# Early even differences, a third pair in turns, and a plain chunk placed elsewhere in a two-layer trunk's ConvFFN

## The chip, the cores and the metric

One core of one Trainium2 chip. The metric is the device time of one execution in microseconds (us), the median of several runs.

## What is computed

A trunk of two layers on 512 tokens of 1024 features, in float32. Layer 0 is a Mamba-2 mixer, layer 1 a differential attention with shared keys and values; behind each stands a ConvFFN, and the change lies in these two.

```python
def conv_ffn(x, ln_g, up_w, conv_w, conv_b, down_w):
    u = causal_dwconv(rms_norm(x, ln_g) @ up_w, conv_w, conv_b)   # 3 taps along the tokens
    gate, up = u[..., :FFN_DIM], u[..., FFN_DIM:]                 # FFN_DIM = 2816
    return (jax.nn.silu(gate) * up) @ down_w
```

## The kernel before

**Products.** float32 products run on TensorE in three passes: each operand is split into a rounded high part (ScalarE) and the rest, its low part (VectorE), and high times high, high times low and low times high are summed in PSUM. Weights come by chunks of 128 x 1024 numbers (512 KB). `chunk(key)` emits loads and splits up to two chunks ahead of the one in use; the tiles `wr` (raw), `wh` and `wl` (high and low) have three buffers each. `plan` lists the chunks in the order of their use.

**Who sets the order.** TensorE runs its instructions in the order of the program. The order of the other engines and of the DMA queues is laid out when the kernel is built, by a planner that takes the program's order as priority and estimates times; an instruction that is ready early can be placed far ahead of its place in the code. Each engine then runs its list strictly in order.

**The up projection.** The 2816 features of gate and of up form 22 pairs of 128 columns each: pair p is gate block p and up block p. Parts `PARTS_D` hold pairs 0-5, 6-13 and 14-21. Two neighbouring pairs form a double. A plain double ("P" in `KINDS`) takes four chunks, gate and up of each pair, in 24 products of 512 tokens each (three passes over eight blocks of x). A double of kind "S" is multiplied in seven half-size products by a Strassen scheme, "5126734", each with 24 products of 256 columns (12 for each of two column blocks); the sums of weights that it needs are added by DMA into the raw tile (`up_plus`, on GpSimd's queue) after an earlier of the seven has read it. `STEPS[i]` is the order of the steps of part i: P a plain chunk, a digit a step of the Strassen double, D the down projection of the part before. Part 1 has two plain doubles (pairs 6-7, 10-11) and two Strassen ones (8-9, 12-13).

**Start of the ConvFFN.** Pairs 0 and 1 are multiplied by x before its norm is known (the row `nr` is multiplied in at evacuation). For the others x is normalised and split in four quarters, `split_whole`: blocks 0 and 2, 1 and 3, then 4 and 6, 5 and 7 (`xgh`, `xgl`). Pairs below `WHOLE` are multiplied in turns: the first chunk holds blocks 0-3 of x's features for the gate columns and the up columns, the second blocks 4-7 for both, so that two PSUM banks grow together. Pairs from `WHOLE` on take the gate chunk with all eight blocks, then the up chunk. `x_sums` forms the sums of x for the Strassen doubles in `sE` and `sO`.

**After a pair.** `taps` forms the three-tap convolution (one ScalarE pass, two VectorE passes) for gate and up, Silu is taken on ScalarE, `gated` multiplies (line 1160) and calls `operands`. The down projection is a Strassen scheme too: of each double it needs seven sides of 256 tokens, split in high and low (`pieces`): side 0 from the even pair, sides 1 to 6 once the odd pair is gated. In layer 0 these are the even pair's difference and the mixed differences and sums, in the tiles `sh` and `sl`; in parts with eight pairs the last double puts them in the tiles of `sE`, which the trace then names `sEh` and `sEl`. `down_features` (layer 0) takes the steps "5126743" with sides 3, 0, 1, 6, 4, 5, 2: the even pair's difference comes first, with 24 products for each of its two chunks in parts of eight pairs.

**Staging.** In layer 0, `stage()` is called once per step and moves key weights for layer 1: at every second call it either loads a tile (SyncE's queue) or scales it on ScalarE (line 1011) and sends it to DRAM (ScalarE's queue). There are eight such tiles, one buffer.

## Time and profile before

| | us |
|---|---|
| median of 3 runs | 1331.74 (1331.48 to 1332.08) |
| profiled execution | 1334.15 |
| its span, first to last instruction | 1332.5 |
| TensorE busy | 1312.7 (99% of the span), mean granted clock 0.992 |
| VectorE busy | 1072.4 (80%) |
| ScalarE busy | 745.8 (56%) |

Lines with L are lines of the kernel. In a wait "X <- Y", engine and tile X stood idle until Y had ended. In rows in order of time, the bracket at the end gives the idle time before the instruction and what ended it.

### The profile page before, as it was taken

The numbers are of one execution on the slowest core, as the hardware profiler recorded it, in microseconds if no ns is written. First come the engines' busy times: TensorE is split into PE (matmuls) and PEld (weight loads), VectorE is DVE, ScalarE is ACT, GpSimd is POOL, SyncE is SP. The second block draws the span as 40 slices with busy tenths as digits, with TensorE's granted clock in tenths as the row PEclk, the third lists the DMA queues.
The fourth block names the chain that finished last, engine by engine and source line by source line (L and its number), as shares of the span: only waits on it lengthen the run. The fifth ranks groups of instructions, "written<-read, shape, count | busy, mean of one in ns | idle before, by whom it ended". The sixth has DMA issues, their size and how long they took to land.

```text
span 1332.5 us, 18904 instructions
## 1 busy us (share of the span) xinstructions
PE 1312.7 (99%) x7059; PEld 1112.0 (83%) x7059; DVE 1072.4 (80%) x1785; ACT 745.8 (56%) x1223; POOL 185.2 (14%) x212
## 2 busy tenths in 40 slices
PE   9999999999999999999998999999999999999998
PEld 8878888888887899889888988778787889978887
DVE  7989888789878977786766969677779978897777
ACT  6696554742456635553444676777656545553442
POOL 4230300300120421011002310000020031011001
PEclk9999999999998999999998999999999999999999
DMA  7553433432365797468336583222143487456335
GB/s 206 158 156 92 143 106 106 140 95 72 118 192 177 169 230 165 121 127 205 98 92 111 162 165 116 80 64 79 49 119 92 114 209 170 127 112 204 95 64 126
DMA packets 198524, 174.18 MB, mean 131 GB/s; under 512 B 7900, under 2 KB 172128, under 8 KB 198432
## 3 DMA queue, kind: packets, MB, share of 16 engines
q1 hardware_dynamic: 164272, 119.68, 30.2%
q0 software_dynamic: 30704, 47.99, 18.8%
q10 hardware_dynamic: 3456, 5.30, 1.1%
q8 instruction: 55, 0.90, 0.3%
q14 instruction: 37, 0.30, 0.1%
HBM read 166.51 MB, written 6.44 MB: 130 GB/s over the span
## 4 chain that ended last, share of the span: by engine, by line
PE 91%; DVE 5%; ACT 2%; DMA 1%; issue 1%; DVEq 0%; ACTq 0%; SPq 0%
PE ps_in L246 5%; PE ps_in L248 5%; PE ps_in L247 5%; PE ps_g L247 4%; PE ps_g L248 4%; PE ps_g L246 4%; PE ps_u L246 4%; PE ps_u L247 4%; PE ps_u L248 4%; PE ps_s L1434 3%; PE ps_s L1439 3%; PE ps_s L1437 3%; PE ps_s L1333 2%; PE ps_s L1336 2%; PE ps_s L1338 2%; PE ps_o L247 2%
## 5 line engine op out<-in xcount | busy, mean ns | idle before, releaser
L196 DVE TENSOR_TENSOR wl_h<-wr_h,wh_h 128x1024 fp32r<-128x1024 f32 x72 | 88.5, 1231 | 47.8 <-ACT wh_h L185 45.2
L246 PE MATMUL ps_in<-xgh,wh_in 128*128 128x512 f32 x304 | 122.9, 404 | 0.0
L248 PE MATMUL ps_in<-xgh,wl_in 128*128 128x512 f32 x304 | 119.7, 394 | 0.0
L247 PE MATMUL ps_in<-xgl,wh_in 128*128 128x512 f32 x304 | 119.1, 392 | 0.0
L185 ACT ACTIVATE wh_h<-wr_h 128x1024 fp32r<-128x1024 f32 x72 | 76.1, 1058 | 76.0 <-PE ps_g L247 32.8
L247 PE MATMUL ps_g<-xgl,wh_h 128*128 128x512 f32 x288 | 113.9, 395 | 3.6 <-DVE xgl L1084 3.6
L248 PE MATMUL ps_g<-xgh,wl_h 128*128 128x512 f32 x288 | 113.6, 395 | 2.3 <-DVE wl_h L196 2.3
L246 PE MATMUL ps_g<-xgh,wh_h 128*128 128x512 f32 x288 | 113.9, 395 | 0.8 <-ACT xgh L1083 0.8
L246 PE MATMUL ps_u<-xgh,wh_h 128*128 128x512 f32 x288 | 112.6, 391 | 0.0
L247 PE MATMUL ps_u<-xgl,wh_h 128*128 128x512 f32 x288 | 112.5, 391 | 0.0
L248 PE MATMUL ps_u<-xgh,wl_h 128*128 128x512 f32 x288 | 112.3, 390 | 0.0
L1238 POOL DMA_DIRECT2D wz<-in_ffn_down_w_dram x28 | 33.8, 1216 | 305.3 <-DVE wl_s L1277 202.4
L1083 ACT ACTIVATE sh<-vg 128x512 fp32r<-128x512 f32 (+1 forms) x72 | 40.2, 571 | 56.2 <-DVE vg L1160 35.9
L247 PEld LDWEIGHTS ps_g<-xgl,wh_h 128*128 128x128 f32 x288 | 54.9, 191 | 15.8 <-DVE xgl L1084 4.9
L1276 ACT ACTIVATE wh_s<-wz 128x1024 fp32r<-128x1024 f32 (+2 forms) x38 | 37.3, 981 | 54.2 <-DMA wz<-in_ffn_down_w_dram 15.0
L248 PEld LDWEIGHTS ps_in<-xgh,wl_in 128*128 128x128 f32 x304 | 57.1, 188 | 12.1 <-issue 0.4
L246 PEld LDWEIGHTS ps_in<-xgh,wh_in 128*128 128x128 f32 x304 | 57.2, 188 | 11.8 <-issue 1.3
L248 PEld LDWEIGHTS ps_g<-xgh,wl_h 128*128 128x128 f32 x288 | 54.8, 190 | 14.2 <-DVE wl_h L196 2.8
L247 PEld LDWEIGHTS ps_in<-xgl,wh_in 128*128 128x128 f32 x304 | 57.2, 188 | 11.0 <-issue 0.5
L246 PEld LDWEIGHTS ps_g<-xgh,wh_h 128*128 128x128 f32 x288 | 54.8, 190 | 12.7 <-ACT xgh L1083 1.7
L1439 PE MATMUL ps_s<-sl,wh_s 128*128 128x256 f32 x252 | 65.2, 287 | 0.0
L1437 PE MATMUL ps_s<-sh,wh_s 128*128 128x256 f32 x252 | 65.1, 286 | 0.0
(512 smaller groups left out, 3787.5 us busy)
## 6 DMA issues: line engine op xcount, KB each, us to landing
wr_h<-in_ffn_up_w_dram SPq DMA_DIRECT2D x64, 512.0 KB, 4.0
wr_in<-in_ssm_in_w_dram SPq DMA_DIRECT2D x40, 512.0 KB, 3.8
wz<-in_ffn_down_w_dram POOLq DMA_DIRECT2D x21, 512.0 KB, 5.7
m<-cumd POOLq DMA_DIRECT2D x16, 512.0 KB, 4.2
wr_out<-in_ssm_out_w_dram SPq DMA_DIRECT2D x16, 512.0 KB, 3.5
wr_s<-in_ffn_down_w_dram SPq DMA_DIRECT2D x13, 512.0 KB, 3.6
wx<-in_ffn_down_w_dram POOLq DMA_DIRECT2D x12, 512.0 KB, 6.5
xT<-in_ffn_up_w_dram POOLq DMA_DIRECT2D x10, 512.0 KB, 7.8
```

The lines of the kernel that those rows point to most:

```text
L185: return act.activation(self.wh[:, :self.n], self.raw[:, :self.n], AF.Copy)
L196: return eng.tensor_tensor(out=self.wl[:, :self.n], in0=self.raw[:, :self.n], in1=self.wh[:, :self.n].bitcast(F32), op=ALU.subtract)
L246: pe.matmul(ps, wh, xh, start=start, stop=False)
L247: pe.matmul(ps, wh, xl, start=False, stop=False)
L248: return pe.matmul(ps, wl, xh, start=False, stop=stop).ins
L1083: act.activation(hi, v, AF.Copy)
L1238: state["plus"] = pool.dma_start(view(t, nq), source(p0, c, nq, j, i), accum_op=ALU.add).ins
L1276: act.activation(wh[:, :n], t[:, :n], AF.Copy)
L1333: pe.matmul(pss[b], h, ws[q][1][:, cols], start=False, stop=end and q == qs[-1], skip_group_check=more)
L1434: pe.matmul(v[:, b], wl[:, q, cols], h, start=False, stop=q == nq - 1, skip_group_check=not opens or b > 0)
L1437: pe.matmul(v[:, b], wh[:, q, cols], h, start=opens and q + b == 0, stop=False, skip_group_check=not opens or b > 0)
L1439: pe.matmul(v[:, b], wh[:, q, cols], w, start=False, stop=False, skip_group_check=not opens or b > 0)
```

## The change

Five edits.

1. `WHOLE` goes from 2 to 3: pair 2 of both layers is multiplied in turns like pairs 0 and 1, its two chunks loaded by two DMAs of 256 KB each.
2. In part 0 of layer 0, `stage()` is called for pairs 4 and 5 only, no longer for pair 3: two calls fewer.
3. In `operands`, layer 0: the even pair's difference is formed and split right after its side 0. It overwrites the even pair's first half.
4. Accordingly the odd pair no longer forms it, and splits the remaining mixed difference alone (256 columns instead of 512).
5. `STEPS[1]`, both layers: a plain chunk that stood between steps 6 and 7 of the second Strassen double now stands between 6 and 7 of the first. The plain chunks keep their order among themselves, so pair 10's second chunk and both of pair 11's each come one place earlier.

```diff
-STEPS = "PPPPPPPPPPPP", "PPDPP51P26734P51P26P734", "PPDPPPPPPPPPPPPPP"
-WHOLE = 2
+STEPS = "PPPPPPPPPPPP", "PPDPP51P26P734P51P26734", "PPDPPPPPPPPPPPPPP"
+WHOLE = 3
...
                     pieces(sh[:, 0], sl[:, 0], h[:, 0])
+                    if not l:
+                        dve.tensor_tensor(out=h[:, 0], in0=h[:, 0], in1=h[:, 1], op=sub)
+                        pieces(sh[:, 3], sl[:, 3], h[:, 0])
                     return
...
                 else:
-                    dve.tensor_tensor(out=e0, in0=e0, in1=e1, op=sub)
                     dve.tensor_tensor(out=e1, in0=o1, in1=e1, op=sub)
...
-                pieces(sh[:, 3:5], sl[:, 3:5], e)
+                if l:
+                    pieces(sh[:, 3:5], sl[:, 3:5], e)
+                else:
+                    pieces(sh[:, 4], sl[:, 4], e1)
...
                         next(sums, None)
-                        if not l:
+                        if not l and p > 3:
                             stage()
```

## The prediction

> **What bounds the kernel now.** I read the page first, then the waits of TensorE by stretch, then the instructions in order of time around each wait, and the busy time of the engines by windows.

> ```profile
> span 1332.5 us, 18904 instructions
> PE 1312.7 (99%) x7059; PEld 1112.0 (83%) x7059; DVE 1072.4 (80%) x1785; ACT 745.8 (56%) x1223; POOL 185.2 (14%) x212
> ...
> PE ps_s L1437 <- ACT sEh L1083: 6.2, 2, 4.8
> PE ps_g L247 <- DVE xgl L1084: 2.8, 2, 2.0
> PE ps_g L248 <- DVE wl_h L196: 2.3, 1, 2.3
> PE ps_s L1439 <- DVE sEl L1084: 0.6, 2, 0.4
> ```

> TensorE is busy 99% of the span, so a change that leaves its products alone can win only what TensorE loses: waits, and products at a lower clock. The wait rows (us in total, times, longest) are those of 390 to 760 us, which holds layer 0's ConvFFN. They come to some 12 us, in four places, and each edit has to do with one of them. I price a place by the time between the start of its step and the start of the next, less what the same products take undisturbed. Rows in order of time begin with start and duration; rows of windows give the window, its length, then busy time and count of TensorE, its weight loads, VectorE, ScalarE and GpSimd, and TensorE's granted clock.

> **Place 1: pair 2 of layer 0 (400 us).** Edit: WHOLE 2 to 3, and stage() from pair 4 on.

> ```profile
> 400.19 0.39 PE L246 MATMUL ps_g<-xgh,wh_h 128*128 128x512 f32 x1
> ...
> 403.56 0.50 PE L246 MATMUL ps_g<-xgh,wh_h 128*128 128x512 f32 x1 [0.36 <-ACT xgh L1083]
> 404.87 0.50 PE L247 MATMUL ps_g<-xgl,wh_h 128*128 128x512 f32 x1 [0.81 <-DVE xgl L1084]
> ...
> 407.84 0.79 PE L247 MATMUL ps_g<-xgl,wh_h 128*128 128x512 f32 x1 [1.99 <-DVE xgl L1084]
> 408.43 0.63 PE L248 MATMUL ps_g<-xgh,wl_h 128*128 128x512 f32 x1
> 408.86 0.63 PE L246 MATMUL ps_g<-xgh,wh_h 128*128 128x512 f32 x1
> ...
> 417.83 0.39 PE L246 MATMUL ps_g<-xgh,wh_h 128*128 128x512 f32 x1
> ...
> 423.27 0.39 PE L246 MATMUL ps_u<-xgh,wh_h 128*128 128x512 f32 x1
> ...
> 401.22 1.34 ACT L1011 ACTIVATE stage<-stage,c 128x512 f32<-128x512 f32 x2 [3.78 <-DMA stage<-in_kv_w_dram]
> 406.56 1.22 DVE L1084 TENSOR_TENSOR xgl<-wx,xgh 128x1024 fp32r<-128x1024 f32 x1
> 400.00:424.00 24.00, 20.84 (x78) 15.92 (x77) 20.47 (x29) 14.80 (x21) 0.19 (x1) 0.86 0.49 158
> 424.00:448.00 24.00, 24.00 (x108) 19.87 (x107) 22.83 (x35) 17.15 (x24) 3.46 (x4) 1.00 0.80 215
> ```

> A chunk of 24 products takes 423.27-417.83 = 5.44 us. Pair 2 has 48, so 10.88, and took 17.64: 6.76 us lost. The waits shown explain 3.2; after the last one the products start 0.43 us apart instead of 0.227 (408.43 to 408.86), which is the rest. The gate chunk runs through all eight blocks of x, and blocks 4 to 7 are not split yet. In turns, the first chunk needs blocks 0 to 3 alone, for both banks, and block 4 is wanted at 400.19+5.44 = 405.63, block 5 with its low part some seven products later, at 407.2. The low part of blocks 5 and 7 ends at 406.56+1.22 = 407.78. So 0.55 us of wait is left if VectorE does the same at the same times. Against it: SP issues two loads for a chunk where it issued one (pairs 0 and 1 do so already, without a wait on them), and both banks are now evacuated at the pair's end, at 400.19+10.88 = 411.07; the old gate chunk, stalled, ended no sooner (24 products before 417.83 are 412.4). I count neither.

> What is late next is VectorE: in the two windows above its busy time is 20.5 and 22.8 of 24 us, and TensorE would arrive some 6 us earlier at the low halves of the weights of pairs 3 to 6. Idle VectorE time in 400 to 448 is 4.7 us, part of it wait for TensorE. Bounds of the gain: 6.8 and 0 (a new wait behind every pair). Of 6.76, 0.55 stays, and 6.2 us earlier against 4.7 us of idle time leaves VectorE 1.5 us short: 4.7. I take 4.5, since not all of that idle time can be filled.

> The two stage() calls dropped shift the staging of key weights by two steps. ScalarE stood 3.78 us in front of the copy at 401.22, with the splits of blocks 4 to 7 queued behind it. The transfers run far ahead of the code (this one starts while pair 1 is multiplied, though its call stands after pair 3), so two steps need not move it. Bounds: 0, and 2 (the 0.55 and the 1.5); I take 0.

> **Place 2: the plain chunk inside the second double (539 us).** Edit: STEPS.

> ```profile
> 539.32 0.40 PE L246 MATMUL ps_g<-xgh,wh_h 128*128 128x512 f32 x1
> ...
> 542.28 0.50 PE L248 MATMUL ps_g<-xgh,wl_h 128*128 128x512 f32 x1 [2.33 <-DVE wl_h L196]
> ...
> 548.99 0.28 PE L1185 MATMUL ps_U<-xgh,wh_U 128*128 128x256 f32 x1
> ...
> 540.41 0.68 DVE L1160 TENSOR_TENSOR vg<-vg,vu 128x512 f32<-128x512 f32 x1
> ...
> 508.00:524.00 16.00, 16.00 (x114) 15.04 (x113) 11.26 (x15) 7.75 (x11) 2.26 (x2) 1.00 0.43 114
> 528.00:544.00 16.00, 13.67 (x83) 11.96 (x82) 16.00 (x26) 12.10 (x20) 2.12 (x2) 0.97 0.75 133
> ```

> Lost: 548.99-539.32-5.44 = 4.23 us. VectorE is full from 528 to 544: the first double has just ended and pair 10, whose second chunk stands behind it, is tapped and gated at the same time (540.41 is its gate, directly ahead of the late weights). With the chunk moved between the first double's 6 and 7, pair 10 ends inside that double, where VectorE has 4.7 of 16 us free, and only half of pair 11 stands behind the double. That takes four taps less a half's two, and a gate, out of the crowd: about 2 x 0.74 + 0.68 = 2.2 us with place for a piece more, against a wait of 2.33. It just covers it; but the first double itself gets 5.44 us later and its own gating stands undiminished ahead of the next plain weights. Bounds: +4.2, and -2 (a wait of the same size at the first double's 7, 3 or 4, half of it beyond what goes). I take 2.3.

> **Place 3: the start of part 1's down projection (580 us).** Edits: early difference, and STEPS.

> ```profile
> 579.75 0.28 PE L1437 MATMUL ps_s<-sh,wh_s 128*128 128x256 f32 x1
> ...
> 582.02 0.38 PE L1437 MATMUL ps_s<-sEh,wh_s 128*128 128x256 f32 x1 [1.40 <-ACT sEh L1083]
> ...
> 589.28 0.28 PE L1437 MATMUL ps_s<-sh,wh_s 128*128 128x256 f32 x1
> ...
> 579.24 0.42 DVE L1314 TENSOR_TENSOR vg<-vg 128x256 f32<-128x256 f32 x1
> 564.00:584.00 20.00, 18.23 (x107) 15.94 (x107) 20.00 (x34) 14.02 (x22) 2.57 (x2) 1.00 0.41 102
> ```

> The first step, m=5, reads side 3, the even pair's difference. It is formed at 579.24 and split only together with the odd pair's side (one piece of 512 columns). m=5 is 48 products of 256 columns; 12 of them take 1.44 us undisturbed, so 5.76; it took 9.53: 3.77 lost. Pair 11's gating, part of what fills VectorE in the window above, moves ahead with its chunk, and the piece no longer waits for the odd pair. It is needed six products after the start. I take 3.4 of 3.77; bounds 0 and 3.8.

> **Place 4: the start of layer 0's last down projection (700 us).** Edit: early difference.

> ```profile
> 700.03 0.28 PE L1437 MATMUL ps_s<-sh,wh_s 128*128 128x256 f32 x1
> ...
> 705.72 0.58 PE L1437 MATMUL ps_s<-sEh,wh_s 128*128 128x256 f32 x1 [4.83 <-ACT sEh L1083]
> ...
> 711.77 0.28 PE L1437 MATMUL ps_s<-sh,wh_s 128*128 128x256 f32 x1
> ...
> 713.21 0.28 PE L1437 MATMUL ps_s<-sh,wh_s 128*128 128x256 f32 x1
> ...
> 694.63 0.43 DVE L1314 TENSOR_TENSOR vg<-vg 128x256 f32<-128x256 f32 x1
> 703.80 0.69 DVE L1160 TENSOR_TENSOR vg<-vg,vu 128x512 f32<-128x512 f32 x1
> ```

> Here the difference is ready at 695.06 and waits ten us for pair 21's gate (703.80). Split at once, it is there five us before 700.03. Lost now: 713.21-700.03-5.76 = 7.42 us (12 products from 711.77 to 713.21 give the 1.44). Late next would be side 1, from pair 21's gate: m=2 wants it 11.5 us after the start, at 711.5, and two passes of some 0.7 us after 704.5 give it. I take 6.9; bounds 5 and 7.4.

> **Layer 1** gets pair 2 in turns and the new STEPS, not the difference.

> ```profile
> 1006.34 0.39 PE L246 MATMUL ps_g<-xgh,wh_h 128*128 128x512 f32 x1
> ...
> 1013.57 0.39 PE L246 MATMUL ps_u<-xgh,wh_h 128*128 128x512 f32 x1
> ```

> 1013.57-1006.34-5.44 = 1.79 lost; I take 1.4, bounds 0 and 1.8. STEPS moves no wait there that I can name: 0, between +0.5 and -2.

> **What the early piece adds.** A split of 512 columns becomes two of 256, in 11 doubles: VectorE 0.42 for a piece of 256 against some 0.69 for 512, so 0.15 a double, 1.7 us in all, ScalarE about the same, spread over 300 us and beside TensorE's work except where priced above. 0.

> **The clock rule.** In place 1 a wait of 1.99 us is followed within a product by starts 0.43 us apart. [...]

> **Sum.** 4.5+2.3+3.4+6.9+1.4 = 18.5 us, of at most 24 (6.8+4.2+3.8+7.4+1.8). The profiled execution took 1334.15 us (span 1332.5), 2.4 above the median of the runs, 1331.74; it becomes 1315.7, and the median 1313.2.

> **Rivals.**
> 1. VectorE becomes the bound behind pair 2 and around the doubles. For it: 22.8 of 24, 16 of 16 and 20 of 20 us busy. Against: much of that work is not due at once. Places 1 and 2 then give nothing, and one more clock drop costs what place 2's did, 4.23-2.33 = 1.9: 18.5-4.5-2.3-1.9 = 9.8, 1322.
> 2. The difference is formed early in the code but stays behind other work on VectorE, as at 579.24. Place 3 gives nothing and place 4 half: 18.5-3.4-3.5 = 11.6, 1320.
> 3. The half clock has another cause than these waits, and stays when they go. What each place lost beyond the waits shown is 3.6+1.9+2.4+2.6 = 10.5 of 22.2 us, so 8.1 of the 17.1 that I count there: 10.4 is left, 1321. Every slow stretch begins right at a wait, so little speaks for it. [...]
> 4. Slower. The second double's 2, 6, 7, 3, 4 now follow without a plain chunk between, and 7 reads a tile to which a DMA must add after step 1's weights. In layer 1 that add is issued at 1130.87 and lands in some 7.8 us; 7's weights are read at 1146.91, or 5.44 earlier, at 1141.5: 2.8 us to spare. It costs from landings over 10.6 us on; it would take 18.5 us over both layers, so two landings near 20 us with their clock drops, say 1336.

> ```profile
> 1130.87 1.29 POOL L1124 DMA_DIRECT2D xT<-in_ffn_up_w_dram  x1 [2.49 <-DVE wl_U L1153]
> 1146.91 1.06 ACT L1152 ACTIVATE wh_U<-xT 128x1024 fp32r<-128x1024 f32 x1 [0.89 <-ACT vg L1066]
> xT<-in_ffn_up_w_dram POOLq DMA_DIRECT2D x10, 512.0 KB, 7.8
> ```

> **How the numbers follow.** Forecast (gain 15 to 23) 0.62; rival 1 0.17; rival 2 0.07; rival 3 0.03; new waits that cancel the gain to within 0.2% (2.7 us, about what a measurement can tell) 0.05; slower 0.06. Faster by over 0.2%: 0.89. Range: 1309 is 22.7 of the at most 24 us; 1324, three above rivals 1 to 3, takes them in, and leaves out the last two and the forecast's extremes, under 2 in 10.

> **What would show it.** Right: no wait on sEh in the list of TensorE's waits; pair 2's 48 products in 11 to 13 us; the chunk after the first double within 5.5 to 7; TensorE's clock at 1.00 in the windows around. Wrong: waits on wl_h, wl_U or wl_s of over 1.5 us between 400 and 460 or 520 and 560, or ScalarE's copy of the staged weights still waiting ahead of xgh.

## The result and the profile after

The changed kernel took 1314.0 us in the median (1312.79 to 1315.6), the kernel before 1331.64 (four runs here, the three of the table above and one more): a ratio of 0.9868, 95% interval 0.9851 to 0.9885, some 17.6 us. The forecast was 1313.2 us and faster. The profiled execution after took 1313.98 us, its median, where the profiled one before stood 2.4 us above its own median; so the spans of the two traces differ by more, 1332.5 to 1312.3, 20.2 us.

The page of the changed kernel: its span, the engines' busy time, and the engines' shares of the chain that ended last.

```profile
span 1312.3 us, 18936 instructions
PE 1303.6 (99%) x7059; PEld 1106.3 (84%) x7059; DVE 1073.5 (82%) x1796; ACT 748.4 (57%) x1234; POOL 185.4 (14%) x212
...
PE 95%; DVE 2%; ACT 1%; DMA 1%; issue 0%; DVEq 0%; ACTq 0%; SPq 0%
```

All waits of TensorE, in the whole span (total, times, longest). Those on `sEh` and `sEl` are gone, those on `xgl` have shrunk to 0.2 us (before: 2.8 from 390 to 760 us, 3.6 in the whole span). One wait on `wl_h` of the old size is there, and it is a new one, at another place.

```profile
PE ps_g L248 <- DVE wl_h L196: 2.2, 1, 2.2
PE warm L330 <- DVE ones L257: 1.1, 1, 1.1
PE ps_s L1341 <- DVE vu L1068: 0.4, 1, 0.4
PE po L1886 <- ACT at L1876: 0.4, 1, 0.4
PE ps_g L247 <- DVE xgl L1084: 0.2, 1, 0.2
```

TensorE's rows in order of time, at the starts and ends of the four places, and the one that waited.

```profile
399.45 0.39 PE L246 MATMUL ps_g<-xgh,wh_h 128*128 128x512 f32 x1
...
410.81 0.39 PE L246 MATMUL ps_g<-xgh,wh_h 128*128 128x512 f32 x1
...
432.57 0.39 PE L246 MATMUL ps_g<-xgh,wh_h 128*128 128x512 f32 x1
...
435.37 0.70 PE L248 MATMUL ps_g<-xgh,wl_h 128*128 128x512 f32 x1 [2.18 <-DVE wl_h L196]
...
442.10 0.39 PE L246 MATMUL ps_u<-xgh,wh_h 128*128 128x512 f32 x1
...
541.86 0.40 PE L246 MATMUL ps_u<-xgh,wh_h 128*128 128x512 f32 x1
...
547.32 0.28 PE L1185 MATMUL ps_U<-xgh,wh_U 128*128 128x256 f32 x1
...
572.62 0.28 PE L1442 MATMUL ps_s<-sh,wh_s 128*128 128x256 f32 x1
...
578.38 0.28 PE L1442 MATMUL ps_s<-sh,wh_s 128*128 128x256 f32 x1
...
689.12 0.28 PE L1442 MATMUL ps_s<-sh,wh_s 128*128 128x256 f32 x1
...
694.88 0.28 PE L1442 MATMUL ps_s<-sh,wh_s 128*128 128x256 f32 x1
```

Pair 2's 48 products take 410.81-399.45 = 11.36 us, the plain chunk in the second double 547.32-541.86 = 5.46, the first step of both down projections 5.76, which is the undisturbed time. But the gate chunk of pair 5 takes 442.10-432.57 = 9.53 us, 4.1 more than the 5.44 of its products; there was no such loss in the kernel before. Its chain, from all engines' rows in order of time (last, in brackets: how long the engine stood before the instruction, and for what):

```profile
426.71 0.37 SPq L1005 DMA_DIRECT2D stage<-in_kv_w_dram  x1
...
431.60 1.34 ACT L1011 ACTIVATE stage<-stage,c 128x512 f32<-128x512 f32 x2 [2.77 <-DMA stage<-in_kv_w_dram]
432.84 0.61 ACT L1478 ACTIVATE vg<-vg 128x512 f32<-128x512 f32 x1
433.49 0.69 DVE L1160 TENSOR_TENSOR vg<-vg,vu 128x512 f32<-128x512 f32 x1 [2.06 <-ACT vg L1478]
434.10 1.22 DVE L196 TENSOR_TENSOR wl_h<-wr_h,wh_h 128x1024 fp32r<-128x1024 f32 x1
```

Read from below: the low half of the weights of pair 5's gate chunk stands behind the gate of pair 3 on VectorE (pair 4's up chunk is still being multiplied then); VectorE stood 2.06 us before that gate, so it was not full; it waited for the SiLU; the SiLU was queued on ScalarE behind a copy of staged key weights, and ScalarE stood 2.77 us in front of the copy, for its load. Busy times and clock by windows:

```profile
400.00:424.00 24.00, 23.84 (x106) 19.39 (x105) 23.16 (x38) 18.83 (x29) 0.20 (x1) 1.00 0.55 162
...
432.00:436.00 4.00, 1.82 (x8) 1.19 (x7) 2.51 (x4) 3.24 (x6) 1.35 (x1) 0.94 0.89 275
436.00:440.00 4.00, 4.00 (x13) 3.14 (x12) 4.00 (x8) 2.40 (x4) 3.36 (x2) 0.64 0.79 187
...
528.00:544.00 16.00, 16.00 (x106) 14.67 (x105) 15.94 (x28) 12.97 (x23) 2.56 (x2) 1.00 0.72 140
```

TensorE's clock is 1.00 again at pair 2 and at the doubles, and falls, to 0.64 in the window from 436 to 440, only behind the new wait. From 528 to 544 VectorE is as full as before and TensorE stands nowhere.

### The profile page after: what moved, and what is told of

Its sections match the earlier page's. It is cut to its first block, busy times and chain, and to the rows that moved or that the text cites. A ratio compares the mean times of both kernels' runs of the same rounds, so it can differ in the third digit from the quotient of the medians.

```text
span 1312.3 us, 18936 instructions
## 1 busy us (share of the span) xinstructions
PE 1303.6 (99%) x7059; PEld 1106.3 (84%) x7059; DVE 1073.5 (82%) x1796; ACT 748.4 (57%) x1234; POOL 185.4 (14%) x212
## 4 chain that ended last, share of the span: by engine, by line
PE 95%; DVE 2%; ACT 1%; DMA 1%; issue 0%; DVEq 0%; ACTq 0%; SPq 0%
PE ps_in L246 5%; PE ps_in L248 5%; PE ps_in L247 5%; PE ps_g L248 5%; PE ps_g L246 4%; PE ps_g L247 4%; PE ps_u L246 4%; PE ps_u L247 4%; PE ps_u L248 4%; PE ps_s L1439 3%; PE ps_s L1444 3%; PE ps_s L1442 3%; PE ps_s L1338 3%; PE ps_s L1341 3%; PE ps_s L1343 3%; PE ps_o L247 2%
## 5 line engine op out<-in xcount | busy, mean ns | idle before, releaser
L246 PE MATMUL ps_in<-xgh,wh_in 128*128 128x512 f32 x304 | 122.9, 404 | 0.0
L196 DVE TENSOR_TENSOR wl_h<-wr_h,wh_h 128x1024 fp32r<-128x1024 f32 x72 | 88.4, 1231 | 41.1 <-ACT wh_h L185 38.3
L248 PE MATMUL ps_in<-xgh,wl_in 128*128 128x512 f32 x304 | 119.7, 394 | 0.0
L247 PE MATMUL ps_in<-xgl,wh_in 128*128 128x512 f32 x304 | 119.1, 392 | 0.0
L248 PE MATMUL ps_g<-xgh,wl_h 128*128 128x512 f32 x288 | 112.9, 392 | 2.2 <-DVE wl_h L196 2.2
L246 PE MATMUL ps_g<-xgh,wh_h 128*128 128x512 f32 x288 | 113.2, 393 | 0.0
L247 PE MATMUL ps_g<-xgl,wh_h 128*128 128x512 f32 x288 | 112.8, 392 | 0.2 <-DVE xgl L1084 0.2
L246 PE MATMUL ps_u<-xgh,wh_h 128*128 128x512 f32 x288 | 112.1, 389 | 0.0
L247 PE MATMUL ps_u<-xgl,wh_h 128*128 128x512 f32 x288 | 112.1, 389 | 0.0
L248 PE MATMUL ps_u<-xgh,wl_h 128*128 128x512 f32 x288 | 112.1, 389 | 0.0
L1083 ACT ACTIVATE sh<-vg 128x512 fp32r<-128x512 f32 (+1 forms) x81 | 42.2, 531 | 60.3 <-DVE vg L1160 35.2
L248 PEld LDWEIGHTS ps_in<-xgh,wl_in 128*128 128x128 f32 x304 | 57.1, 188 | 12.1 <-issue 0.4
L246 PEld LDWEIGHTS ps_in<-xgh,wh_in 128*128 128x128 f32 x304 | 57.2, 188 | 11.7 <-issue 1.3
L247 PEld LDWEIGHTS ps_in<-xgl,wh_in 128*128 128x128 f32 x304 | 57.3, 188 | 11.0 <-issue 0.5
L248 PEld LDWEIGHTS ps_g<-xgh,wl_h 128*128 128x128 f32 x288 | 54.4, 189 | 13.9 <-DVE wl_h L196 2.6
L185 ACT ACTIVATE wh_in<-wr_in 128x1024 fp32r<-128x1024 f32 x39 | 41.3, 1058 | 40.9 <-PE ps_in L247 30.0
L247 PEld LDWEIGHTS ps_g<-xgl,wh_h 128*128 128x128 f32 x288 | 54.5, 189 | 11.6 <-DVE xgl L1084 0.6
## 6 DMA issues: line engine op xcount, KB each, us to landing
wr_h<-in_ffn_up_w_dram SPq DMA_DIRECT2D x60, 512.0 KB, 4.3
wr_in<-in_ssm_in_w_dram SPq DMA_DIRECT2D x40, 512.0 KB, 3.8
wz<-in_ffn_down_w_dram POOLq DMA_DIRECT2D x21, 512.0 KB, 5.9
m<-cumd POOLq DMA_DIRECT2D x16, 512.0 KB, 4.3
wr_out<-in_ssm_out_w_dram SPq DMA_DIRECT2D x16, 512.0 KB, 3.5
wr_s<-in_ffn_down_w_dram SPq DMA_DIRECT2D x13, 512.0 KB, 4.4
wx<-in_ffn_down_w_dram POOLq DMA_DIRECT2D x12, 512.0 KB, 6.6
```

Source lines behind the costliest of these rows:

```text
L185: return act.activation(self.wh[:, :self.n], self.raw[:, :self.n], AF.Copy)
L196: return eng.tensor_tensor(out=self.wl[:, :self.n], in0=self.raw[:, :self.n], in1=self.wh[:, :self.n].bitcast(F32), op=ALU.subtract)
L246: pe.matmul(ps, wh, xh, start=start, stop=False)
L247: pe.matmul(ps, wh, xl, start=False, stop=False)
L248: return pe.matmul(ps, wl, xh, start=False, stop=stop).ins
L1083: act.activation(hi, v, AF.Copy)
```

## The experiments

The table holds, for each kernel, the time from the first product of a stretch to the first of the next, from the starts in its trace: the 288 plain products of pairs 1 to 6 (place 1 lies in them), the plain chunk behind the second double's first steps (2), the down projection of part 1 (3) and the last one (4) of layer 0; then the median and the ratio to the kernel before with its interval. The stretches come from one trace each. The kernel before was run again beside each group of runs; its median there was 1332.4 (the first three single edits and the spread copies), 1333.2 or 1332.5 us, and ratios and gains go by that median, not by the 1331.7 of the first row.

| kernel | 288 plain | 2 | 3 | 4 | median | ratio |
|---|---|---|---|---|---|---|
| before | 72.16 | 9.67 | 44.09 | 47.74 | 1331.7 | 1 |
| changed | 69.96 | 5.46 | 40.31 | 40.31 | 1314.0 | 0.9868 (0.9851-0.9885) |
| early difference alone | 71.16 | 9.22 | 40.68 | 40.31 | 1321.2 | 0.9917 (0.9903-0.9930) |
| WHOLE (and stage) alone | 67.62 | 9.70 | 44.09 | 47.73 | 1327.3 | 0.9963 (0.9951-0.9976) |
| STEPS alone | 70.99 | 5.47 | 40.74 | 47.94 | 1324.1 | 0.9937 (0.9925-0.9950) |
| changed, stage() from pair 3 | 67.88 | 5.47 | 40.31 | 40.31 | 1312.7 | 0.9851 (0.9837-0.9864) |
| changed, copies spread | 65.39 | 5.57 | 40.31 | 40.31 | 1318.5 | 0.9900 (0.9885-0.9915) |
| changed, copies behind pairs 3 to 5 | 67.19 | 5.47 | 40.31 | 40.31 | 1324.9 | 0.9938 (0.9926-0.9950) |
| changed, copies on GpSimd | 74.45 | 5.47 | 40.31 | 40.31 | 1328.9 | 0.9972 (0.9962-0.9982) |
| changed, copies in the last part | 65.39 | 5.47 | 40.31 | 40.31 | 1309.0 | 0.9825 (0.9812-0.9839) |
| the same with WHOLE = 2 | 68.32 | 5.46 | 40.32 | 40.32 | 1313.6 | 0.9857 (0.9842-0.9872) |
| before, copies in the last part | 68.37 | 9.54 | 44.08 | 49.56 | 1331.6 | 0.9992 (0.9983-1.0001) |
| before, waits filled | 71.77 | 9.72 | 42.60 | 46.08 | 1329.4 | 0.9975 (0.9964-0.9987) |

**Each edit alone.** The difference (edits 3 and 4), then WHOLE with the condition on stage() (edits 1 and 2), then STEPS (edit 5), each on the kernel before; their main lines:

```diff
+                    if not l:
+                        dve.tensor_tensor(out=h[:, 0], in0=h[:, 0], in1=h[:, 1], op=sub)
+                        pieces(sh[:, 3], sl[:, 3], h[:, 0])
...
-WHOLE = 2
+WHOLE = 3
...
-STEPS = "PPPPPPPPPPPP", "PPDPP51P26734P51P26P734", "PPDPPPPPPPPPPPPPP"
+STEPS = "PPPPPPPPPPPP", "PPDPP51P26P734P51P26734", "PPDPPPPPPPPPPPPPP"
```

> The early difference alone, on the kernel before. Theory A (four separate stalls of TensorE, each a wait and a stretch at the lower clock behind it): place 4, the last down projection of layer 0, gives 7.4 us and place 3, the start of part 1's down projection, up to 3.8, with 3.4 taken: 10.8 us, 1320.9; its first step at both places then takes 5.8 us, and the stalls of pair 2 (some 400 us) and of the second double (539 us) stay as they were. Rival (the piece is formed early in the code but stays behind other work on VectorE as long as STEPS is the old one): place 3 gives nothing, place 4 alone: 7.4 us, 1324.3.

> WHOLE=3 with stage() from pair 4 on, alone, on the kernel before. Theory A: pair 2 of layer 0 gives 6.3 us, of which a new stall of 4.1 us at pair 5's gate chunk takes most back, as in the changed kernel; layer 1 gives 1.8: net 4.0 us, 1327.7. Rival (the new stall of the changed kernel comes from all three edits together, by VectorE's work): no stall at pair 5 here, 8.1 us, 1323.6.

> The new STEPS alone, on the kernel before. Theory A: the chunk in the second double was 4.2 us over and is so no more; place 3 (the start of part 1's down projection) gives 0 to 1, since the difference is still split with the odd pair's side; layer 1 within 0.5: 4.2 to 5.2 us, 1327.0. Rival (place 3 was cured by STEPS, because pair 11's gating is out of the way, and not by the early difference): 4.2 + 3.4 = 7.6 us, 1324.1.

The difference gave 11.2 us, as the theory had it: place 4 gained 7.4 and place 3 3.4, alone. STEPS gave 8.3, and there the rival was right: place 3 gains 3.4 from STEPS alone too. Either edit is enough for nearly all of it; together they give 3.8.

WHOLE gave 5.1 and fell between the two: the stretch of 288 lost 2.3 us, most of it at a wait of 1.19 us in pair 5's gate chunk, instead of the 4.7 in the changed kernel. There the planner had put the SiLU of pair 3 ahead of the late copy. ScalarE's rows of that run:

```profile
429.65 0.63 ACT L1473 ACTIVATE vg<-vg 128x512 f32<-128x512 f32 x1 [0.73 <-DVE vg L1068]
...
433.72 0.72 ACT L1011 ACTIVATE stage<-stage,c 128x512 f32<-128x512 f32 x1 [1.85 <-DMA stage<-in_kv_w_dram]
```

So the copy held up no gate there, and the wait that is left is VectorE's: it was busy without a gap, and the low half of the weights stood behind its other work, though the high half was ready at 428.26.

```profile
408.00:432.00 24.00, 24.00 (x108) 19.87 (x107) 24.00 (x37) 18.58 (x26) 0.00 (x0) 1.00 0.62 186
...
433.21 1.21 DVE L196 TENSOR_TENSOR wl_h<-wr_h,wh_h 128x1024 fp32r<-128x1024 f32 x1
```

That chunk took 6.92 us, 1.5 more than its products: with this edit alone, what the prediction had put late next, at the price that it had put on it. A full VectorE is not enough for such a wait, though. In the two runs below that have no loss in this stretch it is just as full (24.00 us from 408 to 432); what stands ahead of the weights in its list decides.

The three medians' gains sum to 24.6 us against 17.6 together. 3.0 of that is place 3, counted twice (3.4 and 3.4 alone, 3.8 together); 2.3 is what WHOLE has more alone than in company (67.62 against 69.96); the other 1.7 is within the intervals. Where no edit touches it, the 288 products took between 70.99 and 72.16 us: such is the spread of one profile.

**stage() from pair 3 again.** `if not l and p > 3` becomes `if not l`.

> The changed kernel with stage() called from pair 3 on, as in the kernel before, instead of from pair 4 on. The prediction counted this edit at nothing. Theory A: the stall at pair 5's gate depends on which copy ScalarE meets there and how late its load is; the copies are planned far ahead of the code, so the stall stays, by more or less: within 2.5 us of the changed kernel, 1311.5 to 1316.5. Rival C (the edit was needed: with the earlier calls a copy stands ahead of the splits of x again, as at 401 us in the kernel before): place 1 loses its whole gain, 2.2 us slower than the changed kernel or more.

The edit that I counted at nothing is worth nothing that these runs tell: the intervals of the two ratios overlap, and the median without it is, if anything, the lower. Rival C is out: pair 2's 48 products take 11.47 us there. The wait at pair 5 is still there, 1.56 us instead of 2.18, and without the lower clock behind it: 1.00 from 430 to 442 us (the last section has the windows).

**Where the copies stand.** The next four move the staging of the eight key weights, and nothing else: the copies, and with them the loads and stores around them. Spread over layer 0, each copy behind the latest SiLU of a gate:

```diff
+            with tc.issue_after(state["silu"]):
                 act.activation(v[:, k], v[:, k], AF.Copy, scale=c2[:, 32 + k0 + k:33 + k0 + k])
...
-                act.activation(ga, ga, AF.Silu)
+                state["silu"] = act.activation(ga, ga, AF.Silu).ins
```

> The changed kernel, with each copy of staged key weights on ScalarE queued behind the latest SiLU of a gate at the point where the code calls it, so that the eight copies no longer run between 355 and 433 us but over all of layer 0. Theory A (the new stall at pair 5's gate chunk, 4.1 us, is ScalarE standing 2.8 us in front of a copy whose load is late, with the gate's SiLU behind it): the stall goes, that chunk takes 5.4 to 6 us, 4.1 us less than the changed kernel: about 1310. Rival B (VectorE is the bound behind pair 2, rival 1 of the prediction): the stall stays there or moves by a pair, within 1.5 us of the changed kernel: about 1313.5.

At pair 5 the theory held: 65.39 us for the 288 products, nothing lost. But the kernel became slower, since the same thing happened in the second double. ScalarE's rows:

```profile
530.04 1.34 ACT L1012 ACTIVATE stage<-stage,c 128x512 f32<-128x512 f32 x2 [8.34 <-DMA stage<-in_kv_w_dram]
531.29 0.40 ACT L1084 ACTIVATE sh<-vg 128x256 fp32r<-128x256 f32 x1
...
531.60 1.04 ACT L1153 ACTIVATE wh_U<-wz 128x1024 fp32r<-128x1024 f32 x1
```

ScalarE stood 8.34 us for a load, with the weights of a Strassen product (`wh_U`) queued behind. TensorE waited 2.9 us for `wh_U` and 1.8 for `wl_U`; the 48 products from 532.69 took 13.12 us instead of 5.75.

Behind the gates of pairs 3 to 5, the rest free:

```diff
-                        if not l and p > 3:
-                            stage()
+                        if not l and p > 2:
+                            state["pin"] = True
+                            stage()
+                            stage()
+                            state["pin"] = False
...
+            with tc.issue_after(state["silu"]) if state.get("pin") else nullcontext():
                 act.activation(v[:, k], v[:, k], AF.Copy, scale=c2[:, 32 + k0 + k:33 + k0 + k])
```

> The changed kernel with the copies of staged key weights queued behind the SiLU of the gates of pairs 3, 4 and 5 for the first three, and left free after that, so that the eight copies run some 45 to 60 us later than in the changed kernel, up to the start of the doubles. Theory A: a load that is issued 10 us ahead of a copy that stands behind a gate's SiLU has landed by then, so pair 5 is clean: 4 us faster than the changed kernel, about 1309.5, and up to 2 us of that is lost if the last copies reach into the first double. Rival B: within 1.5 us of the changed kernel.

Both theories missed the time: 1324.9. Pair 5's gate chunk was clean, as theory A had it. But 1.8 us were lost at pair 6's, where ScalarE stood 3.90 us for a load of weights (at 441.33) ahead of a SiLU; and the copies that were left free met the down projection of part 0, where chunks of weights are wanted close behind one another: 43.26 us instead of 30.23.

```profile
468.68 1.34 ACT L1012 ACTIVATE stage<-stage,c 128x512 f32<-128x512 f32 x2 [6.68 <-DMA stage<-in_kv_w_dram]
470.53 0.84 ACT L1277 ACTIVATE wh_s<-wr_s 128x768 fp32r<-128x768 f32 x1 [0.52 <-ACT stage L1012]
...
471.43 0.58 PE L1443 MATMUL ps_s<-sh,wh_s 128*128 128x256 f32 x1 [3.48 <-ACT wh_s L1277]
```

On GpSimd:

```diff
-            act.activation(v[:, k], v[:, k], AF.Copy, scale=c2[:, 32 + k0 + k:33 + k0 + k])
-        act.dma_start(key_weights(k0, i), v)
+            pool.tensor_scalar(out=v[:, k], in0=v[:, k], scalar1=c2[:, 32 + k0 + k:33 + k0 + k], scalar2=None, op0=ALU.mult)
+        pool.dma_start(key_weights(k0, i), v)
```

> The changed kernel with the staged copies, and the stores behind them, on GpSimd instead of ScalarE. The loads are late as before, but it is GpSimd that stands in front of them, with nothing of TensorE's queued behind it before the doubles. Theory A: pair 5's gate chunk without a stall, 4 us faster than the changed kernel, about 1309.5, if GpSimd's copies do not slow VectorE. Rival B: the gate is late all the same, by VectorE: about 1313.

14 us slower than the changed kernel, which neither theory had: "nothing of TensorE's queued behind it" was wrong. GpSimd adds squares for the norm there (`nacc_f`), and these now stood behind the copies:

```profile
385.51 3.11 POOL L1011 TENSOR_SCALAR stage<-stage,c 128x512 f32<-128x512 f32 x2 [4.25 <-DMA stage<-in_kv_w_dram]
388.60 1.25 POOL L605 TENSOR_TENSOR nacc_f<-nacc_f,nsq_f 128x512 f32<-128x512 f32 x1
...
436.01 1.06 ACT L185 ACTIVATE wh_h<-wr_h 128x1024 fp32r<-128x1024 f32 x1 [9.39 <-DMA wr_h<-in_ffn_up_w_dram]
```

TensorE waited 7.79 us for that sum. Its other wait, 6.67 us for `wl_h` at 439.70, is the last row's: a load of weights was late. It was issued right behind a staging load on SyncE's queue, at 429.82, and that one at 429.35; the single staging buffer is free only when the store of the last copy is through, and that store was issued at 426.11.

All in the last part, where plain chunks alone are multiplied:

```diff
-                        if not l and p > 3:
-                            stage()
...
-                    if not l:
-                        stage()
+                    if not l and i == 2:
+                        stage()
+                        stage()
```

(with the copies behind the SiLU, as in the spread run).

> The changed kernel with the staging of key weights moved whole into the last part of layer 0's up projections (some 560 to 690 us), two calls of stage() a step, each copy on ScalarE queued behind the latest gate's SiLU. Nothing is staged near pair 5, nor in the doubles. Theory A (every stall that the changed kernel and the run with the copies spread over layer 0 showed is ScalarE standing in front of a copy whose load is late): pair 5's gate chunk takes 5.4 us, as in the spread run, the doubles stay clean, as in the changed kernel, and the last part has time, since its weights alone are loaded there: 4.6 us faster than the changed kernel, about 1309. Rival B (the stalls come from the sum of VectorE's and ScalarE's work, and move with the copies): a new stall of 2 to 4 us in the last part, about 1313.

1309.0 us, as theory A had it. The 288 products, the doubles and the down projections are without a loss. It is the fastest kernel here: its ratio's interval lies wholly below the changed kernel's, and its span is 5.0 us shorter. Its page (span, and the chain that ended last by engine), then the waits of TensorE:

```profile
span 1307.3 us, 18953 instructions
...
PE 98%; ACT 1%; DVE 1%; issue 0%; DVEq 0%
```

```profile
PE warm L330 <- DVE ones L257: 1.1, 1, 1.1
PE ps_s L1342 <- DVE vu L1069: 0.4, 1, 0.4
PE po L1886 <- ACT at L1876: 0.4, 1, 0.4
```

These runs move the loads and stores along with the copies. That it is the copy, at the head of ScalarE's list, and not the traffic, is read from the chain of rows above, not from the move alone.

**Was place 1 a matter of the copies alone?** The same move on the kernel before, and the last kernel with `WHOLE = 2`.

> The kernel before, with nothing changed but the staging of key weights, moved into the last part of layer 0's up projections. Theory A (place 1 too was ScalarE standing 3.78 us in front of a copy, with the splits of x's blocks 4 to 7 behind it; the order of the third pair's columns only hid that): the splits come some 5 us earlier, pair 2's 48 products take 11 us and the stretch of 288 products some 65.4 instead of 72.2; places 2, 3 and 4 and layer 1 as before: 6.8 us, 1325.5. Rival (the gate chunk of eight blocks is too early for the splits in any case, since VectorE forms their low halves): place 1 keeps 3 us or more of its loss, 1329 or more.

> The run with the staging in the last part, with WHOLE=2 again, so that pair 2 runs through its two columns one after the other. Theory A: without copies on ScalarE in that stretch the splits of blocks 4 to 7 are in time in layer 0, whatever the order of the columns; layer 1 gives back 1.8 and gets 0.7: 1.1 us slower than with WHOLE=3, 1310.2. Rival (the turns are needed as well): 3 us or more slower, 1312 or more.

Theory A falls here, by half, and both rivals' bounds were met: place 1 keeps 3 us of its loss, and without the turns the last kernel is over 4 us slower. Without copies the stretch of 288 still takes 68.37 us on the kernel before and 68.32 on the other, 3 more than with the columns in turns: TensorE waits 1.4 and 0.8 us for the low halves of blocks 4 to 7, which VectorE, busy throughout, forms among taps and a gate. So of place 1's loss of 6.8 us some 3.8 were the copy's and some 3.0 the order of the columns, by one trace each (with a spread of 1.2 us, see above), and the turns are needed as well: without them 0.9857 instead of 0.9825. On the kernel before the move alone brought nothing that the interval tells from zero: the wait at place 4 grew from 4.83 to 6.11 us. ScalarE's rows put its last copy, 1.34 us at 694.91, ahead of pair 21's tap for the up columns, on which that pair's gate waits; that this is the reason is argued, not tried.

**Is the half rate the wait's?** Additional products in front of the two first steps, which the first real one overwrites:

```diff
+                        if m == "5" and c == 0:
+                            for _ in range({6: 16, 14: 44}.get(p0, 0)):
+                                pe.matmul(v[:, 0], wh[:, 0, :P], sides[0][0][:, 0, :], start=True, stop=True,
+                                          skip_group_check=True)
```

> The kernel before, with additional products (overwritten by the first real one) in front of the first step of two down projections of layer 0: 16 of them, 1.92 us, at place 3 and 44, 5.28 us, at place 4, so that TensorE has work where it waited 1.78 and 5.06 us for the difference. Nothing comes earlier. Theory A (the half rate behind a wait is caused by the wait): the real products run at full rate; the first step takes 1.92 + 5.76 = 7.7 us at place 3 instead of 9.5 and 5.28 + 5.76 = 11.0 at place 4 instead of 13.2: 4 us faster, 1328. Rival 3 of the prediction (the half clock has another cause): the real products stay at half rate for as long as before, no gain, 1332 or more.

Faster, with more products: 3.1 us in the median, 1.5 at place 3 and 1.7 at place 4 in the trace, where 4 were expected in all. The rest, 0.4 us at place 3 and 0.5 at place 4, was lost in front of the side's low half, `sEl`, which came later than the end of the fill (0.24 of it is a wait on record). The granted clock is 1.00 in both windows; over the same windows of the kernel before it was 0.83 and 0.79.

```profile
579.00:589.00 10.00, 9.88 (x81) 9.60 (x80) 10.00 (x16) 5.63 (x7) 4.31 (x4) 1.00 0.69 105
698.00:714.00 16.00, 15.76 (x131) 15.52 (x130) 11.48 (x16) 6.69 (x8) 2.58 (x2) 1.00 0.60 93
```

The side that the real products wait for came no earlier, and they ran at full rate. Rival 3 is out for these two places.

## Why the prediction came out, point by point

- **Place 1**, 4.5 taken, 2.2 in the profile. Pair 2 itself was right: 11.36 us, 11.43 by the prediction (10.88 + 0.55). The step that failed is "what is late next is VectorE", priced at 1.5 us. That held with WHOLE alone (1.5 us); in the changed kernel late next was ScalarE, through a staged copy, and with the half rate behind the wait it cost 4.1. The prediction had the row (ScalarE 3.78 us in front of a copy) and looked only at what it did to pair 2. Two of its own signs for a failure came true: a wait on `wl_h` of over 1.5 us between 400 and 460 (2.18 us at 435.37), and the copy that still stood ahead of `xgh` (3.48 us at 400.18), which did no harm there. A small misreading: the old gate chunk of pair 2 ended at 411.42, where its up chunk starts, not at 412.4; nothing hangs on it.
- **Place 2**, 2.3 taken, 4.2 measured: the upper bound. The new wait at the first double did not come.
- **Place 3**, 3.4 taken, 3.8 measured. The prediction put both edits to it; either alone gives 3.4.
- **Place 4**, 6.9 taken, 7.4 measured. The side is split by 686.3, as rows of VectorE show, and the step starts at 689.12.
- **Layer 1**, 1.4 taken, 2.1 measured: pair 2 gave 1.8 (67.18 to 65.39), the first down projection lost 0.7 at a new wait of 0.41 us on `vu` (28.56 to 29.25), and STEPS gave 1.0 at part 1's (39.10 to 38.08). "No wait that I can name" missed the last: a wait of 0.55 us on `vu` stood there.
- **The early piece**, 0 taken: VectorE's busy time rose by 1.1 us, hidden.
- **The sum**: 2.2 + 4.2 + 3.8 + 7.4 + 2.1 = 19.7 of 20.2 us between the spans, against 18.5 forecast; place 1 was 2.3 short, the others 3.5 over. The stretch also started earlier, at 388.46 instead of 389.19, which is more than the rest. That the total came within 1 us of the forecast (17.6 us between the medians) is in part luck: errors of both signs cancelled.
- **Rivals.** 1: in the changed kernel the wait at pair 5 was not VectorE's, which stood 2.06 us, and the stall went when the staging alone was moved. 2: the difference is planned early. 3: out, by the filled waits. 4: no wait on `wl_U` or `wh_U` in either layer.

## What to carry to other kernels

A small job off the main path, put by a planner into an in-order engine's list, stops that engine for as long as its load is late (2.77 us of ScalarE's time in the changed kernel, 8.34 with the copies spread); look at each wait of an engine that is half idle for what is queued behind it, and move the job to a stretch where nothing is, before moving it to another engine. When an edit takes away one wait, ask of every other in-order list in the next 30 us what it stands for, not only of the busiest engine. Price a wait of TensorE with the lower clock behind it: where the clock fell, that was a further 1.9 to 3.6 us here.

## What the runs showed of the hardware

A wait was followed by a lower clock or not, and its length alone does not tell which: a single wait of 1.56 us (stage() from pair 3) left the clock at 1.00, one of 1.88 us (the early difference alone, at 538 us) and one of 2.18 us (the changed kernel, at 435.37) were followed by 0.50; so were waits of 1.40 and 0.38 us close together (before, place 3), and waits of 1.46 and 0.78 (changed, copies in the last part, WHOLE = 2) left it at 1.00.

```profile
580.62:584.03 3.41, 1.64 (x12) 1.44 (x12) 3.41 (x8) 2.20 (x5) 1.28 (x1) 1.00 0.96 147
584.03:587.45 3.42, 3.42 (x18) 3.42 (x17) 3.42 (x6) 1.47 (x2) 0.15 (x1) 0.50 1.05 158
587.45:590.86 3.41, 3.41 (x31) 3.41 (x30) 2.44 (x3) 1.06 (x1) 2.42 (x2) 1.00 0.53 77
```

The early difference alone, the wait of 1.88 us:

```profile
536.82:540.23 3.41, 1.53 (x10) 1.06 (x9) 3.41 (x7) 2.02 (x4) 0.00 (x0) 1.00 0.00 0
540.23:543.65 3.42, 3.42 (x10) 2.64 (x9) 3.42 (x6) 0.42 (x1) 0.00 (x0) 0.50 0.50 153
```

stage() from pair 3, where the wait of 1.56 us lies across two stretches:

```profile
430.68:434.09 3.41, 2.44 (x11) 1.69 (x9) 1.99 (x3) 2.42 (x5) 0.00 (x0) 1.00 0.94 276
434.09:437.50 3.41, 2.81 (x12) 2.31 (x13) 3.41 (x8) 3.29 (x6) 2.42 (x3) 1.00 0.91 303
437.50:440.91 3.41, 3.41 (x17) 2.83 (x16) 3.41 (x6) 1.35 (x3) 2.84 (x3) 1.00 1.04 159
```

Copies in the last part with WHOLE = 2, where the waits of 1.46 and 0.78 us lie in two (in this run and the one above, the stretches are counted back from a low one at the end of the trace, at 1312.64 and 1307.90 us):

```profile
401.28:404.69 3.41, 1.95 (x9) 1.29 (x8) 3.41 (x6) 0.82 (x2) 0.20 (x1) 1.00 0.00 0
404.69:408.11 3.42, 2.64 (x12) 1.88 (x11) 3.42 (x7) 1.17 (x3) 0.00 (x0) 1.00 0.00 0
408.11:411.52 3.41, 3.41 (x17) 2.83 (x16) 3.41 (x5) 2.10 (x3) 0.00 (x0) 1.00 0.27 74
```

In the kernel before, stretches at full clock in which TensorE worked for 1.54, 1.08 and 0.81 us (from 403.13, 539.67 and 700.09) were followed by half the clock, and so was one with 1.23 in the changed kernel (from 432.09) and the one with 1.53 above; those above with 1.95, 2.44, 2.64 and 2.81 were not. Between them the runs do not agree: 1.64 us (1.77 of 3.41 without work) was followed by 0.50 above; 1.72 us by 1.00 in the kernel before with the copies in the last part, at 694.03; 1.88 by 0.50 with the waits filled, at 402.66. These runs give no limit. Stretches at half the clock with 2.11 and 0.96 us of work (the kernel before, from 406.54, place 1, and 703.50, place 4) and with 2.32 (copies behind pairs 3 to 5, at 495.17) were followed by another; those full of work (3.41 to 3.42 us, the kernel before from 543.08 and 584.03, the changed kernel from 435.50) were not. By an estimate from the starts of products (0.43 us apart instead of 0.227), a stretch at half the clock without a wait in it costs some 1.6 us.

GpSimd's copy of 128x512 took 1.57 us in the median where ScalarE's took 0.71, and once 4.78. While that one and the next ran, from 408.40 on, two of VectorE's four taps took 1.10 and 1.17 us, the other two 0.75 and 0.74; beside the copies from 422.69 on, taps took 0.73 to 0.78. What made the two slower, these rows do not show.
